# Attention values for four query tiles at once, an 8 KB weight pool, and the query's inverse root multiplied on POOL

## The chip, the cores and the metric

The kernel runs on one core of a Trainium2 chip. The core has five engines with queues of their own: TensorE (PE; its weight loads are shown as PEld), VectorE (DVE), ScalarE (ACT), GpSimd (POOL) and SyncE (SP, which here only issues DMAs). Every engine executes its own instructions in order and waits on semaphores for the others. The metric is the device time of one execution in microseconds.

## What is computed

One encoder layer over 1024 tokens of width 1024, all in float32, in three sub-layers with residuals. The first mixes a bidirectional RG-LRU with a multi-head latent attention of 8 heads (96 columns of query and key, 64 of value); then come a memory cross-attention and a convolutional SwiGLU feed-forward network (FFN). The change is mostly about the latent attention:

```python
q = rms_norm(q, q_norm)
k = rms_norm(k, k_norm)
q = concatenate([q[..., :64], apply_rope(q[..., 64:], cos, sin)])
k = concatenate([k[..., :64], apply_rope(k[..., 64:], cos, sin)])
...
def attend(q_blk):                       # 8 blocks of 128 queries
    s = einsum('bhqd,bhkd->bhqk', q_blk, kh) * 96 ** -0.5
    p = softmax(s, axis=-1)
    return einsum('bhqk,bhkd->bhqd', p, vh)
```

Norm and rotation leave a factor that belongs to the query's row, the inverse root of its mean square. It may be multiplied into the query, or into the row of scores.

## The kernel before

Every float32 operand of a matmul is split into a rounded hi part and the rest, lo, and a product is made of three matmuls (`mm3`: hi·hi, hi·lo, lo·hi). Weights come through the pool `wp`: a `raw` tile (two buffers) is loaded by SP, and `wsplit` (L125) makes hi and lo of it, on POOL (L134 and L135) or on ACT and DVE. Each is a tile of 1024 columns under the tag "w", of which there are twelve. The two gate tiles (`gate_zero`, L181), the transposed memory rows `mT`, the memory's keys and values `kvr`, the transposed probabilities `pT` and the weights of the FFN's last matmul (`dhi`, `dlo`) take slots of the same tag.

The order of the instructions on each engine isn't written by hand. The context is opened with `schedule_with_timeline_sim=True`: a scheduler with a timeline of its own sets it while the program is built. So a change of a pool can move instructions of stages that it doesn't touch. In the first 60 us the kernel normalises and transposes x (hT), loads the pieces of w_in in the order `w_first`, `w_second`, and on, and projects (psin); beside that, POOL works out the decay factors of the RG-LRU (`sp`).

The attention is a loop over 64 turns, 8 heads by 8 query tiles of 128. For a query tile s:

- `scores(s)`: six matmuls into psS (two PSUM buffers of 1024 columns, pool `pb2`). DVE takes the row maximum into `st` (L754) and multiplies it with the query's inverse root `rq` (L756); ACT takes the Exp with that as its bias and `rq` as its scale (L758), and its row sum; DVE takes the reciprocal (L759); POOL scales the probabilities `pr` in place (L760).
- `turn(s)`: PE transposes `pr` in eight blocks into two psT banks (pool `pb1`, four banks in all, which po and the transposes of keys and queries use too); ACT copies the hi part to pT (L776), DVE subtracts for the lo part (L777).
- `values(u, part)`: a unit u is two query tiles. Its 16 matmuls of 256 columns make po, in two parts of eight. ACT copies the hi and lo halves of po to `ot` (L797, L798), and POOL adds them into `mo` (L799).

In the loop, scores run two turns ahead and values two behind. Between the turns, the next head is prepared: `prep_kn` multiplies the key with its inverse root on POOL (L733, L734), `prep_k` and `prep_q` transpose (`tr96`, L712 to L714), and `head_stats` and `head_roots` work out the inverse roots of the next two heads on ACT, DVE (`inv_root`, L545 to L550) and POOL.

Of the kernel before, what the change touches and what calls it, by code (L numbers as in the profile page):

```python
# [21 lines left out]
P = 128  # L22
# [61 lines left out]
def trunk_layer(ctx: ExitStack, tc: tile.TileContext, a: dict, out: bass.AP):  # L84
# [8 lines left out]
    abcd = ExitStack()  # L93
    wp = abcd.enter_context(tc.tile_pool(name="wp", bufs=12, reuse_waits="tile"))
    lrs = ExitStack()
# [29 lines left out]
    def wsplit(raw, n=1024, gains=None, eng="pool"):  # L125
        hi = wp.tile([P, 1024], F32R, tag="w", name="whi")
        lo = wp.tile([P, 1024], F32R, tag="w", name="wlo")
        w = n // len(gains) if gains else n
        for i in range(n // w):
            sl = slice(i * w, (i + 1) * w)  # L130
            if eng == "pool":
                if gains:
                    pool.tensor_scalar(raw[:, sl], raw[:, sl], gains[i], 0.0, ALU.mult, ALU.add)
                pool.tensor_scalar(hi[:, sl], raw[:, sl], 1.0, 0.0, ALU.mult, ALU.add)  # L134
                pool.tensor_sub(lo[:, sl], raw[:, sl], f(hi)[:, sl])  # L135
# [45 lines left out]
    def gate_zero(jj):  # L181

        wg[jj] = wp.tile([P, 1024], F32, tag="w", name="wgate")
        pool.memset(wg[jj], 0.0)
# [408 lines left out]
    def tp_tile(tag, bufs):  # L593
        return lambda shape, name: tp.tile(shape, F32, tag=tag, bufs=bufs, name=name)


    mT = [[wp.tile([P, 4, MEM], F32R, tag="w", name="mT") for _ in range(2)]
          for q in range(2)]

# [59 lines left out]
    def mem_kv_half(n):  # L659
# [12 lines left out]
        for m in range(2):  # L672
            if n == 0:
                kvr.append(wp.tile([P, 1024], F32, tag="w", name="kvr"))
            act.activation(kvr[m][:, n * 512:(n + 1) * 512], pkv[m], AF.Copy)
# [65 lines left out]
    def prep_q(H, n):  # L741
        qTs[H, n] = cp.tile([QKH, 2, 512], F32R, tag="qT", name="qT")
        tr96(hq[H // 2][:, n * 4:n * 4 + 4, H % 2, :], col("q_g")[:QKH], qTs[H, n])

    def scores(s):
# [8 lines left out]
        dve.tensor_reduce(st[:, 0:1], psS, AX.X, ALU.max, negate=True)  # L754
        r = rq[H // 2][:, i, H % 2:H % 2 + 1]
        dve.tensor_scalar(st[:, 1:2], st[:, 0:1], r, None, ALU.mult)  # L756
        pr = cp.tile([P, S], F32, tag="pr", bufs=3, name="pr")
        act.activation(pr, psS, AF.Exp, bias=st[:, 1:2], scale=r, accum_out=st[:, 2:3])  # L758
        dve.reciprocal(st[:, 3:4], st[:, 2:3])  # L759
# [3 lines left out]
    scaled = {}  # L763

    def turn(s):
        qi = s % 2
        if qi == 0:
            pTs[s // 2] = [[wp.tile([P, 4, 2 * P], F32R, tag="w", name="pT") for _ in range(2)] for _ in range(2)]
        pr = prs.pop(s)
        for n in range(2):  # L770
# [3 lines left out]
            pv = ps.rearrange("p (k c) -> p k c", k=4)  # L774
            dh = pTs[s // 2][n][0][:, :, qi * P:(qi + 1) * P]
            act.activation(dh, pv, AF.Copy)  # L776
            dve.tensor_sub(pTs[s // 2][n][1][:, :, qi * P:(qi + 1) * P], pv, f(dh))  # L777

    def values(u, part):

        H, qq = divmod(u, NT // 2)
        p, hh = H // 2, H % 2
        vt = vts[H]
        if part == 0:
            pos_[u] = pb1.tile([P, 512], F32, tag="b1", name="po")
        po = pos_[u][:, :2 * P]
        th, tl = pTs[u][part]
        for k in range(4):
            mm(po, vt[:, part * 4 + k], th[:, k, :], part == 0 and k == 0, False)
            mm(po, vt[:, part * 4 + k], tl[:, k, :], False, part == 1 and k == 3)  # L790
        if part == 0:
            return
        if qq == 0 and hh == 0:
            mla_f[p] = cp.tile([P, S], F32, tag="mo", bufs=2, name="mo")
        mo = mla_f[p]
        ot = cp.tile([P, 2, 2 * P], F32, tag="ot", bufs=1, name="ot")[VD * hh:VD * hh + VD]
        act.activation(ot[:, 0], po[:VD, :], AF.Copy)  # L797
        act.activation(ot[:, 1], po[VD:2 * VD, :], AF.Copy)  # L798
        pool.tensor_add(mo[VD * hh:VD * hh + VD, qq * 2 * P:(qq + 1) * 2 * P], ot[:, 0], ot[:, 1])  # L799
        if qq < NT // 2 - 1 or hh == 0:  # L800
            return
# [19 lines left out]
    for s in range(NQ + 2):  # L821
        H, i = divmod(s, NT)
        if s + 2 < NQ:
            scores(s + 2)
        if s < NQ:
            turn(s)
        if s >= 2:
            values((s - 2) // 2, s % 2)
        with tc.issue_after(scaled[min(s + 1, NQ - 1)].ins):
# [371 lines left out]
    def product(m):  # L1201
# [5 lines left out]
        for i in range(NH):  # L1207
# [66 lines left out]
```

## Time and profile before

| | |
|---|---|
| median of 3 runs | 1427.37 us (1425.83 to 1431.77) |
| profiled execution | 1426.61 us, span 1424.8 us |
| granted PE clock | 0.995 |
| attention | about 262 to 495 us |
| FFN, first and last matmuls | about 754 to 1212 and 1212 to 1425 us |

The times are of whole executions; the profile shows one, with a span that leaves out 1.8 us around it. A page of the profile lists the busy time of each engine, the costliest groups of instructions and the chain of waits that ended last. In a group's row, the name before the arrow is what is written and the names behind it are what is read; behind the bar stand the busy time, the mean of one in ns, and the time that the engine was idle just before these instructions, with the instruction that ended most of it. PE's matmuls overlap, so their mean is longer than the distance from one to the next.

### The profile page before, as it was taken

What the parts mean: (1) busy time and instruction counts of PE and PEld (TensorE: products, weight loads), DVE (VectorE), ACT (ScalarE), POOL (GpSimd) and SP (SyncE); (2) the same over time, 40 slices, a digit from 0 to 9 for tenths busy, and PEclk for the clock granted to TensorE, in tenths of its full rate; (3) what the DMA queues carried; (4) which work ended last, traced back from release to release, by engine and by line L of the source; (5) the groups of instructions that cost most, each with busy time, mean ns of one, the idle gap of its engine ahead of it and who ended that gap; (6) DMA issues with size and microseconds to landing.
All of it is one profiled execution on the core that took longest, in us unless ns stands there. A gap on an engine that the chain in (4) does not pass through costs nothing.

```text
span 1424.8 us, 18309 instructions
## 1 busy us (share of the span) xinstructions
PE 1373.2 (96%) x6832; PEld 1151.6 (81%) x6832; DVE 903.9 (63%) x1242; ACT 601.2 (42%) x954; POOL 562.2 (39%) x591
## 2 busy tenths in 40 slices
PE   6999899998999999999999999999999999999998
PEld 5766698787888888888887888888888888888887
DVE  6678877899998854576645666443443444665553
ACT  5456855687888822454421111111111122433331
POOL 6713474457687610111339998233223300000000
PEclk9999999999999999999999999999999999999999
DMA  6301101100000141101118887321332222666763
GB/s 203 92 24 37 46 31 47 58 1 1 1 1 1 53 169 46 60 1 30 45 62 279 289 300 254 108 96 59 109 98 81 96 77 94 199 224 205 221 192 103
DMA packets 114232, 145.94 MB, mean 102 GB/s; under 512 B 9547, under 2 KB 64096, under 8 KB 114144
## 3 DMA queue, kind: packets, MB, share of 16 engines
q1 hardware_dynamic: 114143, 144.78, 31.4%
q8 instruction: 54, 0.88, 0.3%
q14 instruction: 35, 0.28, 0.1%
HBM read 105.95 MB, written 38.80 MB: 102 GB/s over the span
## 4 chain that ended last, share of the span: by engine, by line
PE 72%; DVE 11%; ACT 7%; POOL 5%; issue 3%; DMA 2%; SPq 1%; POOLq 0%; ACTq 0%; DVEq 0%
PE psup L109 32%; PE psdn L109 8%; PE psdw L109 6%; PE psP L109 6%; PE psq L109 3%; PE psS L109 3%; PE po L109 3%; PE psmo L109 3%; PE psT L773 2%; DVE st L754 2%; DVE pT L777 1%; POOL wlo L135 1%; PE pq L109 1%; ACT pr L758 1%; DMA raw<-in_w_in 1%
## 5 line engine op out<-in xcount | busy, mean ns | idle before, releaser
L109 PE MATMUL psup<-h,whi 128*128 128x512 f32 x1408 | 434.5, 390 | 1.1 <-POOL ws L1188 0.9
L109 PEld LDWEIGHTS psup<-h,whi 128*128 128x128 f32 x1408 | 264.2, 188 | 56.7 <-POOL ws L1188 1.2
L109 PE MATMUL psup<-h,wlo 128*128 128x512 f32 x704 | 274.1, 389 | 0.0
L1162 ACT ACTIVATE gu<-psup,fcw 128x1024 f32<-128x1024 f32 x44 | 53.3, 1212 | 286.2 <-PE psup L109 286.2
L1163 DVE SCALAR_TENSOR_TENSOR gu<-psup,fcw,gu 128x1023 f32<-128x1023 f32 x44 | 56.4, 1281 | 183.7 <-ACT gu L1162 183.7
L1221 DVE TENSOR_TENSOR dlo<-rawd,dhi 128x1024 fp32r<-128x1024 f32 x77 | 93.3, 1223 | 102.2 <-ACT dhi L1220 102.1
L109 PEld LDWEIGHTS psup<-h,wlo 128*128 128x128 f32 x704 | 132.2, 188 | 27.3
L134 POOL TENSOR_SCALAR whi<-raw 128x1024 fp32r<-128x1024 f32 (+2 forms) x58 | 68.2, 1176 | 217.0 <-PE psup L109 178.0
L135 POOL TENSOR_TENSOR wlo<-raw,whi 128x1024 fp32r<-128x1024 f32 (+2 forms) x58 | 142.3, 2454 | 27.8 <-PE psin L109 24.6
L1220 ACT ACTIVATE dhi<-rawd 128x1024 fp32r<-128x1024 f32 x77 | 81.4, 1061 | 158.8 <-PE psdw L109 44.8
L109 PE MATMUL psS<-kT,qT 96*128 96x512 f32 x384 | 103.9, 404 | 3.9 <-ACT pr L758 3.8
L109 PE MATMUL psin<-hT,whi 128*128 128x512 f32 (+1 forms) x288 | 89.0, 393 | 9.5 <-DVE xf L355 8.2
L760 POOL TENSOR_SCALAR pr<-pr,st 128x1024 f32<-128x1024 f32 x64 | 71.8, 1123 | 54.1 <-DVE st L759 32.8
L777 DVE TENSOR_TENSOR pT<-psT,pT 128x512 fp32r<-128x512 f32 x128 | 84.4, 678 | 5.5 <-ACT pT L776 5.4
L758 ACT ACTIVATE pr<-psS,st,rqk 128x1024 f32<-128x1024 f32 x64 | 77.2, 1206 | 18.6 <-DVE st L756 14.2
L754 DVE TENSOR_REDUCE st<-psS 128x1 f32<-128x1024 f32 x64 | 77.6, 1213 | 8.3 <-PE psS L109 6.7
L109 PEld LDWEIGHTS psS<-kT,qT 96*128 96x128 f32 x384 | 67.6, 189 | 17.6 <-ACT pr L758 6.2
L1188 POOL TENSOR_TENSOR ws<-rawd 128x512 f32<-128x512 f32 x55 | 79.4, 1471 | 0.0
L109 PE MATMUL po<-pT,vt 128*128 128x256 f32 x512 | 72.3, 287 | 3.5 <-DVE pT L777 3.3
L776 ACT ACTIVATE pT<-psT 128x512 fp32r<-128x512 f32 x128 | 70.9, 596 | 7.5 <-PE psT L773 6.9
L773 PE MATMUL psT<-ident,pr 128*128 128x128 f32 x512 | 68.3, 273 | 5.7 <-POOL pr L760 3.6
L109 PEld LDWEIGHTS psin<-hT,whi 128*128 128x128 f32 x288 | 54.6, 198 | 23.6 <-issue 6.7
(301 smaller groups left out, 2810.0 us busy)
## 6 DMA issues: line engine op xcount, KB each, us to landing
raw<-in_w_up SPq DMA_DIRECT2D x44, 512.0 KB
rawd<-ad SPq DMA_DIRECT2D x77, 256.0 KB
wd<-ws SPq DMA_DIRECT2D x55, 256.0 KB
ad<-as SPq DMA_DIRECT2D x55, 256.0 KB
rawd<-wd SPq DMA_DIRECT2D x55, 256.0 KB
rawd<-in_w_down SPq DMA_DIRECT2D x22, 512.0 KB
ad<-gu SPq DMA_DIRECT2D x22, 256.0 KB
rawd<-in_w_down SPq DMA_DIRECT2D x22, 256.0 KB
```

The costliest lines, as they stand in the source:

```text
L109: return pe.matmul(ps, lhsT=l, rhs=r, start=start, stop=stop)
L134: pool.tensor_scalar(hi[:, sl], raw[:, sl], 1.0, 0.0, ALU.mult, ALU.add)
L135: pool.tensor_sub(lo[:, sl], raw[:, sl], f(hi)[:, sl])
L754: dve.tensor_reduce(st[:, 0:1], psS, AX.X, ALU.max, negate=True)
L758: act.activation(pr, psS, AF.Exp, bias=st[:, 1:2], scale=r, accum_out=st[:, 2:3])
L760: scaled[s] = pool.tensor_scalar(pr, pr, st[:, 3:4], 0.0, ALU.mult, ALU.add)
L773: pe.transpose(ps[:, i * P:(i + 1) * P], pr[:, (n * 4 + i) * P:(n * 4 + i + 1) * P], ident)
L776: act.activation(dh, pv, AF.Copy)
L777: dve.tensor_sub(pTs[s // 2][n][1][:, :, qi * P:(qi + 1) * P], pv, f(dh))
L1188: pool.tensor_tensor(st, raws[h0][:, c0], raws[h1][:, c1], op)
L1220: act.activation(hi, raw, AF.Copy)
L1221: dve.tensor_sub(lo, raw, f(hi))
```

## The change

There are three edits.

1. The tag "w" of `wp` has six slots of 8 KB a partition in place of twelve of 4 KB. Tiles are allocated in pairs: hi and lo of a weight, both gate tiles, the two tiles of `mT`, of `kvr`, and `dhi` with `dlo`.
2. A unit of the values is four query tiles: 16 matmuls of 512 columns each fourth turn, issued ahead of the transposes of that turn. A pT tile is twice as wide. ACT copies one half of po straight to `mo` and the other to `ot`, and POOL adds `ot` to `mo`.
3. `prep_q` multiplies the query with its inverse root on POOL, in place, ahead of the transposes. The scores then need neither the scale of the Exp nor the multiplied maximum.

```diff
-    wp = abcd.enter_context(tc.tile_pool(name="wp", bufs=12, reuse_waits="tile"))
+    wp = abcd.enter_context(tc.tile_pool(name="wp", bufs=6, reuse_waits="tile"))
...
     def wsplit(raw, n=1024, gains=None, eng="pool"):
-        hi = wp.tile([P, 1024], F32R, tag="w", name="whi")
-        lo = wp.tile([P, 1024], F32R, tag="w", name="wlo")
+        hl = wp.tile([P, 2, 1024], F32R, tag="w", name="whl")
+        hi, lo = hl[:, 0], hl[:, 1]
...
     def gate_zero(jj):
-        wg[jj] = wp.tile([P, 1024], F32, tag="w", name="wgate")
+        if jj == 0:
+            wg["both"] = wp.tile([P, 2, 1024], F32, tag="w", name="wgate")
+        wg[jj] = wg["both"][:, jj]
         pool.memset(wg[jj], 0.0)
...
     def prep_q(H, n):
         qTs[H, n] = cp.tile([QKH, 2, 512], F32R, tag="qT", name="qT")
-        tr96(hq[H // 2][:, n * 4:n * 4 + 4, H % 2, :], col("q_g")[:QKH], qTs[H, n])
+        q = hq[H // 2][:, n * 4:n * 4 + 4, H % 2, :]
+        r = rq[H // 2][:, n * 4:n * 4 + 4, H % 2:H % 2 + 1]
+        pool.tensor_tensor(q, q, r.to_broadcast([P, 4, QKH]), ALU.mult)
+        tr96(q, col("q_g")[:QKH], qTs[H, n])
...
         dve.tensor_reduce(st[:, 0:1], psS, AX.X, ALU.max, negate=True)
-        r = rq[H // 2][:, i, H % 2:H % 2 + 1]
-        dve.tensor_scalar(st[:, 1:2], st[:, 0:1], r, None, ALU.mult)
         pr = cp.tile([P, S], F32, tag="pr", bufs=3, name="pr")
-        act.activation(pr, psS, AF.Exp, bias=st[:, 1:2], scale=r, accum_out=st[:, 2:3])
+        act.activation(pr, psS, AF.Exp, bias=st[:, 0:1], scale=1.0, accum_out=st[:, 2:3])
...
+    NG = 4
+
     def turn(s):
-        qi = s % 2
+        qi = s % NG
         if qi == 0:
-            pTs[s // 2] = [[wp.tile([P, 4, 2 * P], F32R, tag="w", name="pT") for _ in range(2)] for _ in range(2)]
+            pTs[s // NG] = [[wp.tile([P, 4, NG * P], F32R, tag="w", name="pT") for _ in range(2)] for _ in range(2)]
...
-    def values(u, part):
+    def values(u):
...
-        po = pos_[u][:, :2 * P]
-        th, tl = pTs[u][part]
-        for k in range(4):
-            mm(po, vt[:, part * 4 + k], th[:, k, :], part == 0 and k == 0, False)
-            mm(po, vt[:, part * 4 + k], tl[:, k, :], False, part == 1 and k == 3)
-        if part == 0:
-            return
+        po = pb1.tile([P, 512], F32, tag="b1", name="po")
+        for part in range(2):
+            th, tl = pTs[u][part]
+            for k in range(4):
+                mm(po, vt[:, part * 4 + k], th[:, k, :], part == 0 and k == 0, False)
+                mm(po, vt[:, part * 4 + k], tl[:, k, :], False, part == 1 and k == 3)
...
-        ot = cp.tile([P, 2, 2 * P], F32, tag="ot", bufs=1, name="ot")[VD * hh:VD * hh + VD]
-        act.activation(ot[:, 0], po[:VD, :], AF.Copy)
-        act.activation(ot[:, 1], po[VD:2 * VD, :], AF.Copy)
-        pool.tensor_add(mo[VD * hh:VD * hh + VD, qq * 2 * P:(qq + 1) * 2 * P], ot[:, 0], ot[:, 1])
+        hr = slice(VD * hh, VD * hh + VD)
+        mc = mo[hr, qq * NG * P:(qq + 1) * NG * P]
+        ot = cp.tile([P, NG * P], F32, tag="ot", bufs=1, name="ot")[hr]
+        act.activation(mc, po[:VD, :], AF.Copy)
+        act.activation(ot, po[VD:2 * VD, :], AF.Copy)
+        pool.tensor_add(mc, mc, ot)
...
         if s + 2 < NQ:
             scores(s + 2)
+        if s >= NG and s % NG == 0:
+            values(s // NG - 1)
         if s < NQ:
             turn(s)
-        if s >= 2:
-            values((s - 2) // 2, s % 2)
```

The scheduler's order moves with it, at three places that the prediction speaks of. The first is POOL near 28 us, at the second and third piece of w_in (whi and wlo, or whl, are hi and lo; rs is the inverse root of a row of x). Before:

```order
L209 TENSOR_TENSOR xt_113<-xt_113,gba_91 128x1024
L134 TENSOR_SCALAR whi_484<-raw_115 128x1024
L146 TENSOR_TENSOR rs_247<-rs_247,nhalf_80 128x1
L146 TENSOR_TENSOR rs_268<-rs_268,nhalf_80 128x1
L135 TENSOR_TENSOR wlo_485<-raw_115,whi_484 128x1024
L134 TENSOR_SCALAR whi_549<-raw_547 128x1024
L135 TENSOR_TENSOR wlo_550<-raw_547,whi_549 128x1024
```

The same place on POOL with the change:

```order
L211 TENSOR_TENSOR xt_112<-xt_112,gba_91 128x1024
L134 TENSOR_SCALAR whl_483<-raw_114 128x1024
L146 TENSOR_TENSOR rs_246<-rs_246,nhalf_80 128x1
L146 TENSOR_TENSOR rs_267<-rs_267,nhalf_80 128x1
L134 TENSOR_SCALAR whl_547<-raw_545 128x1024
L135 TENSOR_TENSOR whl_483<-raw_114,whl_483 128x1024
L135 TENSOR_TENSOR whl_547<-raw_545,whl_547 128x1024
```

The hi of the third piece now stands ahead of the lo of the second. The memset of the second gate tile, which stood between the fifth and the sixth piece, has moved to the start of POOL's queue, and the gate's eight DMAs on SP ahead of the load of the fourth piece.

The second place is DVE in the first head of the attention. Before:

```order
L754 TENSOR_REDUCE st<-psS 128x1
L549 SCALAR_TENSOR_TENSOR t_2276<-t_2276 128x16
L759 RECIPROCAL st<-st 128x1
L777 TENSOR_TENSOR pT<-psT,pT 128x4x128
L756 TENSOR_SCALAR st<-st,rqk 128x1
L550 SCALAR_TENSOR_TENSOR rqk<-t_2276 128x2x8
L777 TENSOR_TENSOR pT<-psT,pT 128x4x128 x2
```

DVE there with the change (L760 is the maximum, L763 the reciprocal, L783 the subtraction for pT):

```order
L760 TENSOR_REDUCE st<-psS 128x1
L783 TENSOR_TENSOR pT<-psT,pT 128x4x128
L763 RECIPROCAL st<-st 128x1
L551 SCALAR_TENSOR_TENSOR t_2859<-t_2859 128x16
L717 SCALAR_TENSOR_TENSOR qT<-ps_2442,pcols,qT 96x512
L783 TENSOR_TENSOR pT<-psT,pT 128x4x128 x2
```

The multiply of the maximum, which stood three instructions behind it, is gone; what follows the maximum no longer stands ahead of the Exp.

The third is PE in the middle of the attention, for one unit of values. Before:

```order
L109 MATMUL po<-pT,vt 128x256 x9
L109 MATMUL psS<-kT,qT 128x512 x6
L109 MATMUL po<-pT,vt 128x256 x7
L773 MATMUL psT<-ident,pr 128x128 x8
L712 MATMUL ps_3841<-ident,kn 96x128 x4
L109 MATMUL psS<-kT,qT 128x512 x6
```

PE with the change:

```order
L109 MATMUL po<-pT,vt 128x512
L109 MATMUL psS<-kT,qT 128x512 x6
L779 MATMUL psT<-ident,pr 128x128 x4
L109 MATMUL po<-pT,vt 128x512 x8
L779 MATMUL psT<-ident,pr 128x128 x4
L109 MATMUL po<-pT,vt 128x512 x7
L109 MATMUL psS<-kT,qT 128x512 x6
L779 MATMUL psT<-ident,pr 128x128 x8
```

A unit's values are still 16 matmuls, of twice the columns and half as often; scores and transposes of a turn stand between their pieces. On POOL, the 16 new multiplies (L748) stand in pairs: six ahead of the first scaled probabilities, then two each behind the 4th, 11th and 15th and four behind the 43rd and 46th together.

More of the change, by code (lines that the diff above doesn't have):

```diff
@@ L594, in tp_tile @@
         return lambda shape, name: tp.tile(shape, F32, tag=tag, bufs=bufs, name=name)
-    mT = [[wp.tile([P, 4, MEM], F32R, tag="w", name="mT") for _ in range(2)]
-          for q in range(2)]
+    mT = [wp.tile([P, 2, 4, MEM], F32R, tag="w", name="mT") for q in range(2)]
+    mT = [(t[:, 0], t[:, 1]) for t in mT]
     def mem_rows(m):
@@ L672, in mem_kv_half @@
         for m in range(2):
-            if n == 0:
-                kvr.append(wp.tile([P, 1024], F32, tag="w", name="kvr"))
+            if n == 0 and m == 0:
+                kvt = wp.tile([P, 2, 1024], F32, tag="w", name="kvr")
+                kvr.extend((kvt[:, 0], kvt[:, 1]))
             act.activation(kvr[m][:, n * 512:(n + 1) * 512], pkv[m], AF.Copy)
@@ L774, in turn @@
             pv = ps.rearrange("p (k c) -> p k c", k=4)
-            dh = pTs[s // 2][n][0][:, :, qi * P:(qi + 1) * P]
+            dh = pTs[s // NG][n][0][:, :, qi * P:(qi + 1) * P]
             act.activation(dh, pv, AF.Copy)
-            dve.tensor_sub(pTs[s // 2][n][1][:, :, qi * P:(qi + 1) * P], pv, f(dh))
-    def values(u, part):
-        H, qq = divmod(u, NT // 2)
+            dve.tensor_sub(pTs[s // NG][n][1][:, :, qi * P:(qi + 1) * P], pv, f(dh))
+    def values(u):
+        H, qq = divmod(u, NT // NG)
         p, hh = H // 2, H % 2
         vt = vts[H]
-        if part == 0:
-            pos_[u] = pb1.tile([P, 512], F32, tag="b1", name="po")
-        po = pos_[u][:, :2 * P]
-        th, tl = pTs[u][part]
-        for k in range(4):
-            mm(po, vt[:, part * 4 + k], th[:, k, :], part == 0 and k == 0, False)
-            mm(po, vt[:, part * 4 + k], tl[:, k, :], False, part == 1 and k == 3)
-        if part == 0:
-            return
+        po = pb1.tile([P, 512], F32, tag="b1", name="po")
[4 more added lines that the diff above has]
+                mm(po, vt[:, part * 4 + k], tl[:, k, :], False, part == 1 and k == 3)
         if qq == 0 and hh == 0:
@@ L795, in values @@
         mo = mla_f[p]
-        ot = cp.tile([P, 2, 2 * P], F32, tag="ot", bufs=1, name="ot")[VD * hh:VD * hh + VD]
-        act.activation(ot[:, 0], po[:VD, :], AF.Copy)
-        act.activation(ot[:, 1], po[VD:2 * VD, :], AF.Copy)
-        pool.tensor_add(mo[VD * hh:VD * hh + VD, qq * 2 * P:(qq + 1) * 2 * P], ot[:, 0], ot[:, 1])
-        if qq < NT // 2 - 1 or hh == 0:
+        hr = slice(VD * hh, VD * hh + VD)
[4 more added lines that the diff above has]
+        pool.tensor_add(mc, mc, ot)
+        if qq < NT // NG - 1 or hh == 0:
             return
@@ L1217, in product @@
             nc.sync.dma_start(raw[:, 0], ad[m, i])
-            hi = wp.tile([P, 2, 512], F32R, tag="w", name="dhi")
-            lo = wp.tile([P, 2, 512], F32R, tag="w", name="dlo")
+            hl = wp.tile([P, 2, 2, 512], F32R, tag="w", name="dhl")
+            hi, lo = hl[:, 0], hl[:, 1]
             act.activation(hi, raw, AF.Copy)
```

## The prediction

> **What bounds the kernel now.** The page's first part gives busy shares over the whole span:
>
> ```profile
> PE 1373.2 (96%) x6832; PEld 1151.6 (81%) x6832; DVE 903.9 (63%) x1242; ACT 601.2 (42%) x954; POOL 562.2 (39%) x591
> ```
>
> TensorE (PE) is busy for 96% of the span, so a change pays only if it shortens PE's own work or the few microseconds in which PE waits. Edits 2 and 3 work in the attention, which the trace has from about 262 to 495 us. There the windows view (core 0: stretch and its length, then busy time and count of PE, PEld, DVE, ACT and POOL, PE clock, DMA share, GB/s) says how close the other engines are:
>
> ```profile
> core 0: us, PE busy (x) PEld busy (x) DVE busy (x) ACT busy (x) POOL busy (x), PEclk, DMA share, GB/s
> ...
> 300.00:340.00 40.00, 35.86 (x246) 31.57 (x244) 38.10 (x75) 32.45 (x61) 24.88 (x35) 1.00 0.00 1
> 340.00:380.00 40.00, 38.85 (x265) 34.60 (x266) 37.05 (x75) 33.65 (x62) 28.88 (x40) 1.00 0.01 1
> 380.00:420.00 40.00, 36.97 (x249) 32.57 (x248) 38.42 (x80) 32.30 (x61) 34.47 (x49) 1.00 0.00 1
> ```
>
> VectorE (DVE) is busy 37 to 38 of 40 us, and where it reaches 38, PE falls to 36 or 37: PE and DVE share the bound. The groups of that stretch (262 to 495 us; after the bar: busy us, mean ns of one, idle us of the engine just before them and its releasers; a few records are missing, the code has 384, 512, 512 and 64) show what the waits are:
>
> ```profile
> L109 PE MATMUL psS<-kT,qT 96*128 96x512 f32 x372 | 100.8, 405 | 3.9 <-ACT pr L758 3.8
> L777 DVE TENSOR_TENSOR pT<-psT,pT 128x512 fp32r<-128x512 f32 x126 | 83.0, 678 | 5.4 <-ACT pT L776 5.2
> L758 ACT ACTIVATE pr<-psS,st,rqk 128x1024 f32<-128x1024 f32 x64 | 77.2, 1206 | 18.6 <-DVE st L756 14.2 <-DVE t L548 1.9 <-DVE t L546 1.2
> ...
> L109 PE MATMUL po<-pT,vt 128*128 128x256 f32 x495 | 69.6, 288 | 3.5 <-DVE pT L777 3.3
> L773 PE MATMUL psT<-ident,pr 128*128 128x128 f32 x508 | 67.7, 273 | 5.7 <-POOL pr L760 3.6 <-DVE pT L777 1.4 <-ACT ot L798 0.7
> ...
> L799 POOL TENSOR_TENSOR mo<-ot 64x256 f32<-64x256 f32 x30 | 22.5, 750 | 8.8 <-ACT ot L798 4.8 <-PE psT L773 3.1
> ...
> L756 DVE TENSOR_SCALAR st<-st,rqk 128x1 f32<-128x1 f32 x62 | 12.4, 200 | 0.1
> ...
> L733 POOL TENSOR_TENSOR kn<-hp,rqk 128x256 f32<-128x256 f32 x12 | 7.5, 621 | 5.5 <-PE ps L712 5.2
> ...
> L734 POOL TENSOR_TENSOR kn<-krs,rqk 128x128 f32<-128x128 f32 x12 | 4.8, 404 | 0.0
> ```
>
> PE's idle time in the attention is 3.9 + 5.7 + 3.5 = 13.1 us; most of it waits for the Exp (L758) or the scaled probabilities that follow it (L760). The Exp itself idles 18.6 us, and 14.2 of that ends with L756, the small multiply that edit 3 removes. This is the wait that matters.
>
> **Edit 2, the value matmuls.** 512 matmuls of 256 columns become 256 of 512. The chain of waits has undisturbed rows of either width (start, duration, count), and of scores and transposes, needed later:
>
> ```profile
> 284.62 1.39 PE psS L109 x6
> 286.01 1.31 PE psT L773 x12
> ...
> 402.39 1.89 PE po L109 x16
> ...
> 754.49 457.21 PE psup L109 x2016
> ```
>
> A 256-column matmul takes 1.89 / 16 = 118 ns, a 512-column one 457.21 / 2016 = 227 ns (scores: 1.39 / 6 = 232). So 512 x 118 = 60.5 us become 256 x 227 = 58.1: **-2.4 us** of PE work. [...] ACT's and POOL's evictions of the values become half as many at twice the width. The 16 POOL adds of 512 columns take at most twice the 0.75 us of L799, 24 us as now; ACT saves fixed costs, and is not the bound.
>
> **Edit 3, the removed multiply and the new one.** L756 takes 0.2 us, 64 times, 12.8 us of DVE at most. Worse is where it stands. DVE and ACT around 281 us (start, duration):
>
> ```profile
> 280.02 1.21 DVE L754 TENSOR_REDUCE st<-psS 128x1 f32<-128x1024 f32 x1
> ...
> 281.15 0.16 DVE L550 SCALAR_TENSOR_TENSOR t<-t 128x16 f32<-128x16 f32 x1
> 281.24 0.15 DVE L759 RECIPROCAL st<-st 128x1 f32<-128x1 f32 x1
> 281.31 0.66 DVE L777 TENSOR_TENSOR pT<-psT,pT 128x512 fp32r<-128x512 f32 x1
> ...
> 281.90 0.20 DVE L756 TENSOR_SCALAR st<-st,rqk 128x1 f32<-128x1 f32 x1
> ...
> 282.19 1.20 ACT L758 ACTIVATE pr<-psS,st,rqk 128x1024 f32<-128x1024 f32 x1 [2.53 <-DVE st L756]
> ```
>
> The maximum is there at 281.23, but three other DVE instructions are queued between it and L756, and the Exp starts at 282.19. It could have started some 0.1 us behind the maximum (L756 starts at 281.90, lasts 0.20, and the Exp follows 0.09 later): 0.87 us earlier. The order of the instructions has one to three such instructions between nearly every maximum and its L756, often the reciprocal, which itself waits for the Exp before. After the change the Exp waits for the maximum alone. Bounds: nothing, if PE then waits for something else, and all 13.1 us. Of these, 3.9 + 5.7 hang on the Exp and what follows it, and 3.5 on L777, which loses only the 0.2 us ahead of it. I take about nine tenths of the first 9.6: **-8.5 us**. What is late next is DVE itself: 38 of 40 us less 11 turns x 0.2 us (a turn is 233 / 64 = 3.6 us) leaves 36, just under PE's share.
>
> The new POOL multiply has 128x384 elements, 16 times. Rows L734 and L733 give 0.404 us for 128 columns and 0.621 for 256; another 128 by the same step make 0.84 us, 13.4 us in all. POOL has room for it in the first two windows. But four of the 16 stand together behind the 43rd and 46th scaled tile, in the stretch around 380 to 420 us, where POOL is busy 34.47 of 40 us: 34.5 + 4 x 0.84 = 37.8. The scaling of the next tile is queued behind them, and PE's transposes wait for that; the transposes of the query wait for the multiply itself, a new wait. Between 0 (POOL idles enough) and 3.4 us (all four show) I take **+1.0 us**.
>
> One row speaks against more POOL work:
>
> ```profile
> 282.68 0.15 DVE L548 TENSOR_TENSOR t<-rqk,t 128x16 f32<-128x16 f32 x1
> ...
> 323.62 1.13 POOL L760 TENSOR_SCALAR pr<-pr,st 128x1024 f32<-128x1024 f32 x1 [0.53 <-DVE t L545]
> 323.76 1.00 DVE L548 TENSOR_TENSOR t<-rqk,t 128x16 f32<-128x16 f32 x1
> ```
>
> The same small DVE instruction took 0.15 us once and 1.00 us while POOL ran L760, and both ended together. [...]
>
> **Edit 1, the weight pool.** Twelve pieces of 4 KB become six of 8 KB, so a weight's hi and lo share a slot, and so do both gate tiles. The order after shows what that moves, in the first 62 us. POOL now writes the hi of the third weight ahead of the lo of the second. The trace of before at that place (POOL, one DMA of the chain of waits, and ACT at the end):
>
> ```profile
> 27.74 1.05 POOL L134 TENSOR_SCALAR whi<-raw 128x1024 fp32r<-128x1024 f32 x1
> ...
> 29.17 3.98 DMA raw<-in_w_in
> ...
> 29.79 2.54 POOL L135 TENSOR_TENSOR wlo<-raw,whi 128x1024 fp32r<-128x1024 f32 x1
> ...
> 33.23 1.04 POOL L134 TENSOR_SCALAR whi<-raw 128x1024 fp32r<-128x1024 f32 x1 [0.90 <-DMA raw<-in_w_in]
> ...
> 34.36 2.40 POOL L135 TENSOR_TENSOR wlo<-raw,whi 128x1024 fp32r<-128x1024 f32 x1
> ...
> 40.74 1.05 POOL L134 TENSOR_SCALAR whi<-raw 128x1024 fp32r<-128x1024 f32 x1 [0.51 <-DMA raw<-in_w_in]
> ...
> 45.30 0.96 POOL L184 MEMSET wgate<- 128x1024 f32 x1
> ...
> 61.82 0.20 POOL L311 TENSOR_SCALAR sp<-sp 128x8 f32<-128x8 f32 x1
> 62.05 1.24 ACT L388 ACTIVATE av<-thr,sp 128x1024 f32<-128x1024 f32 x1 [8.85 <-POOL sp L311]
> ```
>
> The third weight's DMA lands only at 33.15, so its hi cannot start before 33.23. The lo that ran at 29.79 in POOL's idle time now runs at 34.4 to 36.8, and the third lo to 39.2. Only the end of the second's lo frees its raw buffer: the load issued then (before: 32.3; after: 36.8) lands 4.0 us later, at 40.8. Then hi (1.05) and lo (2.4) of the fourth end at 44.3, where the next hi starts, not at 40.74: 3.6 us late. The second gate memset (0.96) has moved ahead to where POOL idled, so 2.6 remain on POOL's queue until sp, for which ACT waits 8.85 us at 62. The eight gate DMAs that moved ahead of the fourth weight's load on SP's queue take 0.63 us each and are through before its buffer is free. From 62 us on, nothing is fixed in time that could take the shift back: **+2.6 us**, between 0 (other slack) and 4.
>
> **Sum**, against the profiled execution's 1426.6 us (span 1424.8 and 1.8 around it; 0.8 below the median 1427.4): 1426.6 + 2.6 - 2.4 - 8.5 + 1.0 = **1419.3 us**. The out projection, memory attention and FFN, with PE busy throughout, stay as they are.
>
> **Rivals.**
> - All 13.1 us of PE's waits go and POOL costs nothing: 1426.6 + 2.6 - 2.4 - 13.1 = 1413.7. For it: 14.2 us of waits at L756 vanish at their source. Against it: DVE stays nearly as busy as PE.
> - It doesn't do what it says: the Exp starts earlier, but DVE is as busy with the rest and PE's waits move elsewhere. 1426.6 + 2.6 - 2.4 = 1426.8.
> - The slower side: the lump. Values come as 16 matmuls of 3.6 us every fourth turn. In the three turns between, PE has 1.39 + 8 x 0.109 = 2.26 us of work and DVE 1.21 + 2 x 0.68 + 0.15 = 2.72: PE idles 0.46 x 3 = 1.4 us, unless DVE has worked ahead during the lump, which two score buffers allow only in part. It cancels the gain from 0.46 us a unit (7.3 / 16), and at half of 1.4, 11 us over 16 units, with no gain at the Exp, gives 1426.6 + 2.6 - 2.4 + 11 = 1437.8. For it: before, half as large a lump came twice as often. Against it: the order splits it in 9 + 7 or 8 + 7 with transposes or scores between.
>
> **How the numbers follow.** Forecast 0.50, full recovery 0.18, no recovery 0.17, the lump 0.15. About 0.5%, 7.1 us, is what a measurement of this kernel tells from no change: faster means below 1420.2, slower above 1434.5. The forecast's own spread (8.5 by 4 us either way, the early shift by 1.5) puts 0.3 of its 0.5 below 1420.2. Faster: 0.3 + 0.17 = 0.47; same: 0.2 + 0.01 + 0.17 = 0.38; slower 0.15. The range 1409 to 1437 leaves out the ends of the full recovery and of the lump.
>
> **What would show it.** The profile after should have no DVE instruction between maximum and Exp, under 5 us of ACT idle before the Exp, PE idle in the attention near 5 us, value rows near 227 ns apart, and sp about 2.6 us later. Wrong it would be if DVE's busy share stays at 38 of 40 us, if PE idles before psT for POOL, or if PE's idle time sits in the turns without values.

## The result, and the profile after

The changed kernel takes **1450.5 us** (median; 1447.8 to 1451.0) where the kernel before takes 1426.7. The ratio is 1.015, with an interval of 1.012 to 1.017: slower by 24 us, where 7 us faster was forecast, and outside the range of 1409 to 1437. Single slow executions, of 1544 to 3546 us, are left out of all medians below.

The first part of the page (busy us, share of the span, instructions), after:

```profile
PE 1386.3 (96%) x6576; PEld 1142.9 (79%) x6576; DVE 893.7 (62%) x1178; ACT 590.0 (41%) x922; POOL 570.7 (39%) x591
```

It reads almost like the one of before. Places show more than shares. From the timelines and the chains of waits, start of the same instruction in the two traces:

| | before, us | after, us | later by |
|---|---|---|---|
| a row of the up projection (pk, six matmuls) | 204.69 | 210.21 | 5.5 |
| first Exp of the attention | 261.23 | 267.78 | 6.6 |
| 45th Exp | 423.50 | 430.25 | 6.8 |
| 49th Exp | 438.71 | 455.46 | 16.8 |
| 64th (last) Exp | 489.69 | 510.85 | 21.2 |
| out projection, a row of 156 matmuls | 513.14 | 537.34 | 24.2 |
| FFN, the row of 2016 matmuls | 754.49 | 778.58 | 24.1 |

Everything is lost by the start of the out projection, and most of it at three places: 5.5 us ahead of the up projection, 10.0 in the four turns between the 45th and 49th Exp, and 7.4 from there to the out projection. From the first to the 45th Exp both kernels take the same time (162.3 us before, 162.5 after), so the three edits together gained nothing there either.

The groups after, 268 to 515 us, columns as before:

```profile
L783 DVE TENSOR_TENSOR pT<-psT,pT 128x512 fp32r<-128x512 f32 x122 | 80.2, 682 | 30.2 <-ACT pT L782 20.7 <-PE po L109 9.4
L762 ACT ACTIVATE pr<-psS,st 128x1024 f32<-128x1024 f32 x64 | 71.9, 1123 | 14.5 <-DVE st L763 8.4 <-DVE st L760 6.0
L782 ACT ACTIVATE pT<-psT 128x512 fp32r<-128x512 f32 x123 | 68.1, 604 | 30.5 <-PE psT L779 30.1
L109 PE MATMUL psS<-kT,qT 96*128 96x512 f32 x372 | 103.6, 410 | 5.2 <-ACT pr L762 4.8
L779 PE MATMUL psT<-ident,pr 128*128 128x128 f32 x504 | 70.0, 277 | 5.5 <-POOL pr L764 2.6 <-DVE pT L783 1.3 <-ACT ot L803 1.0
L109 PE MATMUL po<-pT,vt 128*128 128x512 f32 x240 | 67.1, 415 | 0.9 <-DVE kT L717 0.5 <-DVE qT L717 0.3
L715 PE MATMUL ps<-ident,kn 128*96 128x128 f32 x56 | 8.9, 283 | 6.8 <-POOL kn L737 6.0 <-DVE t L550 0.8
```

ACT idles 14.5 us ahead of the Exp, not under 5. Its copies of the transposed probabilities now idle 30.5 us, 30.1 of them for PE. On the page of before it was 7.5:

```profile
L776 ACT ACTIVATE pT<-psT 128x512 fp32r<-128x512 f32 x128 | 70.9, 596 | 7.5 <-PE psT L773 6.9
```

DVE's share did fall as forecast, to 33 to 36 of 40 us in the windows from 300 to 420 us. PE's idle time in these rows is 5.2 + 5.5 + 0.9 + 6.8 = 18.4 us, against 13.1 before, and the last row is new: transposes of a key that wait for its scaling on POOL. The windows view (columns as before) and the timeline (start, duration, the wait in brackets) of that place:

```profile
430.00:440.00 10.00, 4.78 (x25) 3.32 (x23) 9.79 (x19) 4.20 (x8) 8.09 (x10) 0.86 0.00 0
440.00:450.00 10.00, 7.95 (x34) 7.05 (x35) 4.33 (x11) 4.14 (x7) 5.54 (x9) 0.63 0.01 2
```

```profile
401.52 1.05 ACT L588 ACTIVATE acct<-mo 128x1024 f32<-128x1024 f32 x1
404.15 2.82 POOL L593 TENSOR_TENSOR acc<-acc,acct 128x256 f32<-128x256 f32 x4
407.69 0.66 ACT L562 ACTIVATE sqk<-hp 128x512 f32<-128x512 f32 x1
...
427.26 0.63 ACT L562 ACTIVATE sqk<-hp 128x512 f32<-128x512 f32 x1
...
429.99 0.60 PE L715 MATMUL ps<-ident,kn 128*96 128x128 f32 x4
...
440.76 0.17 DVE L552 SCALAR_TENSOR_TENSOR rqk<-t 128x16 f32<-128x16 f32 x1
441.02 0.62 POOL L736 TENSOR_TENSOR kn<-hp,rqk 128x256 f32<-128x256 f32 x1 [2.21 <-DVE rqk L552]
441.59 0.40 POOL L737 TENSOR_TENSOR kn<-krs,rqk 128x128 f32<-128x128 f32 x1
442.05 1.09 PE L715 MATMUL ps<-ident,kn 128*96 128x128 f32 x4 [5.97 <-POOL kn L737]
```

PE waits 5.97 us for a key of the last pair of heads, whose inverse roots are ready only at 440.9. The same places in the trace of before:

```profile
393.83 0.16 DVE L550 SCALAR_TENSOR_TENSOR rqk<-t 128x16 f32<-128x16 f32 x1
394.08 1.06 ACT L586 ACTIVATE acct<-mo 128x1024 f32<-128x1024 f32 x1 [0.38 <-DVE st L759]
...
400.16 0.63 ACT L560 ACTIVATE sqk<-hp 128x512 f32<-128x512 f32 x1
...
424.67 0.16 DVE L550 SCALAR_TENSOR_TENSOR rqk<-t 128x16 f32<-128x16 f32 x1
```

The squares of the finished second pair (L586, L588), the statistics (sqk) and the temporaries of the inverse roots (t) share one buffer, the tile acct. Before, the first half of the last pair's statistics and roots was through it at 394.0, then came the squares. With the change, the values are written ahead of the turn, so the squares claim the buffer first, and both halves follow: the second ends at 440.9, not 424.8, where the Exps up to there are only 6.8 us late.

### The profile page after: what moved, and what is told of

Same layout as the page of the kernel before. It is cut to its first block, busy times and chain, and to the rows that moved or that the text cites. A ratio compares the mean times of both kernels' runs of the same rounds, so it can differ in the third digit from the quotient of the medians.

```text
span 1448.9 us, 17645 instructions
## 1 busy us (share of the span) xinstructions
PE 1386.3 (96%) x6576; PEld 1142.9 (79%) x6576; DVE 893.7 (62%) x1178; ACT 590.0 (41%) x922; POOL 570.7 (39%) x591
## 4 chain that ended last, share of the span: by engine, by line
PE 72%; DVE 12%; ACT 9%; POOL 3%; issue 3%; DMA 1%; SPq 1%; ACTq 0%; POOLq 0%; DVEq 0%
PE psup L109 33%; PE psdn L109 8%; PE psdw L109 6%; PE psP L109 6%; PE po L109 4%; PE psq L109 3%; PE psmo L109 3%; PE psS L109 2%; DVE st L760 2%; DVE pT L783 2%; PE psT L779 1%; ACT pT L782 1%; ACT pr L762 1%; PE pq L109 1%; DMA raw<-in_w_in 1%
## 5 line engine op out<-in xcount | busy, mean ns | idle before, releaser
L109 PE MATMUL psup<-h,whl 128*128 128x512 f32 x2112 | 480.7, 389 | 1.1 <-DVE gu L1169 0.9
L109 PEld LDWEIGHTS psup<-h,whl 128*128 128x128 f32 x2112 | 396.2, 188 | 84.0 <-POOL ws L1193 1.2
L135 POOL TENSOR_TENSOR whl<-raw,whl 128x1024 fp32r<-128x1024 f32 (+2 forms) x58 | 144.8, 2498 | 3.3
L1226 DVE TENSOR_TENSOR dhl<-rawd,dhl 128x1024 fp32r<-128x1024 f32 x77 | 93.3, 1223 | 73.0 <-ACT dhl L1225 73.0
L1225 ACT ACTIVATE dhl<-rawd 128x1024 fp32r<-128x1024 f32 x77 | 81.3, 1060 | 117.0 <-PE psdw L109 46.4
L109 PE MATMUL psdn<-dhl 128*128 128x512 f32 x528 | 120.3, 389 | 0.0
L109 PEld LDWEIGHTS psdn<-dhl 128*128 128x128 f32 x528 | 99.1, 188 | 20.5
L109 PE MATMUL psin<-hT,whl 128*128 128x512 f32 (+1 forms) x432 | 101.4, 393 | 13.8 <-DVE xf L357 8.6
L109 PEld LDWEIGHTS psin<-hT,whl 128*128 128x128 f32 x432 | 79.4, 200 | 33.8 <-issue 11.8
L783 DVE TENSOR_TENSOR pT<-psT,pT 128x512 fp32r<-128x512 f32 x128 | 84.0, 682 | 32.4 <-ACT pT L782 23.0
L109 PE MATMUL psdw<-dhl 128*128 128x512 f32 x396 | 90.2, 389 | 0.0
L109 PEld LDWEIGHTS psdw<-dhl 128*128 128x128 f32 x396 | 74.3, 188 | 15.4
L760 DVE TENSOR_REDUCE st<-psS 128x1 f32<-128x1024 f32 x64 | 77.8, 1216 | 7.5 <-PE psS L109 7.3
L762 ACT ACTIVATE pr<-psS,st 128x1024 f32<-128x1024 f32 x64 | 71.9, 1123 | 14.5 <-DVE st L763 8.4
```

The source lines that it names most:

```text
L109: return pe.matmul(ps, lhsT=l, rhs=r, start=start, stop=stop)
L762: act.activation(pr, psS, AF.Exp, bias=st[:, 0:1], scale=1.0, accum_out=st[:, 2:3])
L783: dve.tensor_sub(pTs[s // NG][n][1][:, :, qi * P:(qi + 1) * P], pv, f(dh))
L1226: dve.tensor_sub(lo, raw, f(hi))
```

## The experiments

The theories. Time is lost at places of their own: at the buffer acct and in the early part that edit 1 reorders (letter A in the expectations, where one is named). Rivals: the new multiplies fill POOL and hold up the scaled tiles (D); edit 2 itself costs, by its block of 16 wide value matmuls and the order of the queues that comes with it (C); the probabilities lack a slot (H). Where an expectation gives a letter another meaning, it says so. Each ratio compares a kernel with runs of before that were made beside it. Their medians were 1426.9 to 1427.4, and they spread from 1425 to 1437, so a ratio can differ by 0.1 or 0.2% from that of two medians.

**1. Squares of a finished pair one turn later** (behind the first half of the statistics, as before):

```diff
+        if p < 3:
+            held.append((p, mo))
+        else:
+            pair_done(p, mo)
...
+        if held and s % NG == 1:
+            pair_done(*held.pop())
```

> The changed kernel, with the squares of a finished pair of heads (and what hangs on them) issued one turn later, so that the first half of the statistics of the next pair is again ahead of them in the queue for the single acct tile. Theory A (the acct tile: since values come a turn earlier, the square of the second pair takes the tile before the statistics of the fourth pair, which then start some 10 turns late, and the keys of head 6 are late): the 10 us lost between the 44th and 48th Exp go, PE's 6.0 us wait for kn goes, total about 1440. Rival B (the lump of 16 value matmuls or the fuller POOL starves the others there): no change, about 1450, and the wait stays.

Measured 1440.2 us (ratio 1.008, 1.006 to 1.010): 10.4 less. The key's row in the groups:

```profile
L715 PE MATMUL ps<-ident,kn 128*96 128x128 f32 x56 | 8.5, 273 | 0.8 <-DVE t L550 0.8
```

Its idle time fell from 6.8 to 0.8 us with all multiplies still on POOL, and from the 45th to the 49th Exp it takes 15.0 us (15.2 before, 25.2 in the changed kernel). The order at acct was the cause of these 10 us.

**2 to 4. One edit alone, or one left out.** Edit 1 alone; edit 3 alone; edits 1 and 2 without 3. None needs a line that the diff doesn't have.

> The kernel before with edit 1 alone (six slots of 8 KB, hi and lo in one, pT's hi and lo in one). Theory A (edit 1 costs only in the first 62 us, by POOL's order there, and the shift grows by a collision of POOL and DVE at about 72 us): +5 us at the queries' up projection, about 1432 in all, attention as before. Rival C (the early shift is hidden or comes from the other edits): 1427.

> The kernel before with edit 3 alone (the query multiplied on POOL, no multiply of the maximum). Theory A (the Exp waits for the maximum alone, 13 us of PE's waits are there to be had): 1418 to 1423, PE idle in the attention under 9 us, sp at 62 us as before. Rival D (POOL's 13.4 us of multiplies and its collisions with DVE eat it): 1427 or more.

> The changed kernel without edit 3 (the maximum is multiplied on DVE again, no multiply of the query on POOL): edits 1 and 2 alone. Theory A (the stall near the 44th turn is the acct tile's, and has nothing to do with the multiplies): it stays, some 1450 to 1455. Rival D (the multiplies that stand behind the 43rd scaled tile on POOL make it): the stall goes, 1435 to 1440.

Edit 1 alone: 1437.2 us (1.005, 1.003 to 1.007), twice the loss expected; its up projection is 6.4 us late, the rest is lost in the attention. Edits 1 and 2: 1456.6 us (1.019, 1.016 to 1.023); the squares go first without the multiplies too, and the four turns from the 45th to the 49th Exp take 20.9 us, so POOL's extra work isn't the cause of the stall. Edit 3 as a whole saves 6.1 us beside them (1456.6 - 1450.5). Edit 3 alone: 1432.0 us (1.0029, 1.0013 to 1.0046), not faster but slower. Its groups, 262 to 515 us:

```profile
L774 PE MATMUL psT<-ident,pr 128*128 128x128 f32 x512 | 71.9, 276 | 8.0 <-DVE pT L778 5.9 <-DVE kT L714 2.1
L777 ACT ACTIVATE pT<-psT 128x512 fp32r<-128x512 f32 x128 | 74.8, 598 | 22.7 <-PE psT L774 22.0
L759 ACT ACTIVATE pr<-psS,st 128x1024 f32<-128x1024 f32 x62 | 69.3, 1118 | 15.4 <-DVE st L757 9.1 <-DVE st L760 3.3 <-DVE t L546 1.5
```

The multiply and its wait are gone (14.2 us before), but ACT still idles 15.4 ahead of the Exp, now mostly for the maximum itself (L757), and 22.7 ahead of the copies, where it was 7.5. The timeline shows how, at one place:

```profile
369.58 1.22 DVE L757 TENSOR_REDUCE st<-psS 128x1 f32<-128x1024 f32 x1 [0.46 <-PE psS L109]
...
371.13 1.04 PE L774 MATMUL psT<-ident,pr 128*128 128x128 f32 x8
...
371.77 1.08 ACT L777 ACTIVATE pT<-psT 128x512 fp32r<-128x512 f32 x2 [1.13 <-PE psT L774]
...
372.74 1.12 ACT L759 ACTIVATE pr<-psS,st 128x1024 f32<-128x1024 f32 x1
```

The maximum is done at 370.80. The Exp stands on ACT behind two copies that wait for PE, and starts 1.94 us later. At this place the head of ACT's queue waits for something else now. It is one place, and most of the loss lies elsewhere: from the 36th to the 48th Exp this kernel takes 50.6 us and the one before 42.4, and the inverse roots of the last pair's second half are ready at 433.5 in place of 424.8.

**5. Values in two pieces.** Experiment 1, with the second half of a unit's values held behind the next turn's transposes:

```diff
         if s >= NG and s % NG == 0:
-            values(s // NG - 1)
+            values(s // NG - 1, 0)
         if s < NQ:
             turn(s)
+        if s > NG and s % NG == 1 or s == NQ + 1:
+            with tc.issue_after(last_tr[min(s, NQ - 1)].ins):
+                values(s // NG - 1, 1)
```

> As the first experiment (all three edits, squares one turn later), with a unit's 16 value matmuls in two parts: eight in the turn in which they came, and eight held on PE behind the transposes of the next turn. Theory C (the lump: with 16 value matmuls of 512 columns in one turn PE has too little work in the other three, which costs about 1 us a unit where PE sets the pace): the heads without statistics fall from 29 to 30 us to 28 to 28.5, total 1428 to 1433 (from 1440). Rival F (it isn't the lump but POOL's multiplies and the order on ACT, where copies for pT now stand ahead of a ready Exp): 1438 to 1442.

Measured 1449.1 us (1.014, 1.011 to 1.017): 9 worse than in one piece. The four tiles' probabilities stay in use a turn longer that way, so this neither supports nor rules out the block as a cause.

**6. The early order of before.** Experiment 1, with the two gate tiles apart and the hi of w_in's third piece kept behind the lo of the second:

```diff
+                if len(los) == 1:
+                    with tc.issue_after(los[0].ins):
+                        pool.tensor_scalar(hi[:, sl], raw[:, sl], 1.0, 0.0, ALU.mult, ALU.add)
...
-        if jj == 0:
-            wg["both"] = wp.tile([P, 2, 1024], F32, tag="w", name="wgate")
-        wg[jj] = wg["both"][:, jj]
+        wg[jj] = wp.tile([P, 2, 1024], F32, tag="w", name="wgate")[:, 0]
```

> As the first experiment, with the order of the first 62 us as before: the gate tiles apart (each half an 8 KB slot), and POOL's hi of the third piece of w_in held behind the lo of the second. Theory A (the shift of 5.4 us at the queries' up projection comes from that order alone; POOL's late piece then also stretches DVE's multiply at 72 us): ACT starts av at 62.0 again, the up projection at 204.7, total about 1435. Rival G (pairs of hi and lo cost something wherever they are, or the pool of six starves a load): shift of over 3 us stays, 1438 or more.

Measured 1435.0 us (1.004, 1.003 to 1.006): 5.2 less, and the row of the up projection stands at 204.77, as before. That the early order cost these 5 us is shown. It isn't quite the order of before, though: the factor av, which waits for sp, starts at 58.93 here and not at 62.05, and yet the up projection comes no earlier. So the start of av alone doesn't set it.

**7 to 10. Edits 1 and 3, bare and mended; edit 3 mended; hi first.** "Mended" is with the order of experiment 6 where edit 1 is there, and with the squares two turns later, behind both halves of the statistics. Hi first is experiment 1 with each part's four hi matmuls ahead of its four lo ones. The two changes:

```diff
+        if held and s % 4 == 2:
+            pair_done(*held.pop())
```

```diff
             for k in range(4):
                 mm(po, vt[:, part * 4 + k], th[:, k, :], part == 0 and k == 0, False)
+            for k in range(4):
                 mm(po, vt[:, part * 4 + k], tl[:, k, :], False, part == 1 and k == 3)
```

> The kernel before with edits 1 and 3, values still by two tiles. If the costs of edit 1 (9.8 us) and of edit 3 (4.6 us) add up: 1442, and the wider values, with squares one turn later, are then worth 2 us (1440 in the first experiment). Theory C (the lump costs over 5 us more than the wider matmuls save): 1435 or less.

> As the first experiment, with the eight matmuls of each part of a unit's values in another order: the four of hi, then the four of lo (before: alternating), so that the hi tile of a part is free four matmuls, 0.9 us, earlier. Theory H (five of the six slots are pT's, one is kvr's; a unit needs four, so its last tile takes the hi slot of the other unit's second part, and DVE and ACT wait there for value matmuls): DVE's waits for po fall from 3.9 us to under 1, total 1436 to 1438. Rival C (the lump itself holds the transposes back, slots or not): 1440, or slower.

> Edits 1 and 3 with values by two tiles, the order of the first 62 us as before (as in the sixth experiment), and the squares of a finished pair two turns later, so that both halves of the statistics are ahead of them. Theory A: 5.3 us from the first 62 us and 3 to 4 us from head 5 (33.0 us, whose second half of statistics waits for acct) off 1433.5: 1423 to 1426, faster than before by 1 to 4 us. Rival G (the costs only move on): 1428 to 1434.

> Edit 3 alone on the kernel before, with the squares two turns later as in the run ahead of this. Edit 3 alone lost 8.4 us between the 36th and the 48th Exp, where the second half of the fourth pair's statistics waits for acct. Theory A (that wait is the loss): 1423 to 1426. Rival D (it is POOL's multiplies and the order on ACT): 1430 to 1433 as in the third experiment.

| | us | ratio |
|---|---|---|
| edits 1 and 3 | 1433.5 | 1.0041 (1.0028 to 1.0055) |
| experiment 1, hi first | 1436.8 | 1.0055 (1.0035 to 1.0074) |
| edits 1 and 3, mended | 1426.2 | 0.9988 (0.9972 to 1.0005) |
| edit 3, mended | 1424.3 | 0.9963 (0.9943 to 0.9982) |

The losses of the edits don't add: 9.8 for edit 1 alone and 4.6 for edit 3 alone (against 1427.4), but 6.5 for both (against 1427.0); and edit 2, with the squares moved, costs 6.7 beside them (1440.2 - 1433.5). Hi first gains 3.4 us beside experiment 1. DVE's wait for value matmuls ahead of its subtraction, 3.9 us there, is gone; but the order moved elsewhere too, so the gain can't be laid to one wait. Mended, both edits are even with the kernel before, and edit 3 alone is the one version that measured faster than it, by 0.4%, inside the 0.5% that counted as no change. Moving the squares took the stall away: from the 36th to the 48th Exp it takes 42.7 us. Its profiled execution, the longest of its twelve, is no shorter than that of before (span 1425.2 us, before 1424.8), so the trace doesn't show where the gain lies.

**11. A sixth slot for the probabilities.** One of the six 8 KB slots holds the memory's projected keys and values (kvr) during the attention. Here kvr is filled with ones after the attention, so the memory's own keys and values are left out, and the slot is free. Beside experiment 1:

```diff
+        kvs = wp.tile([P, 1024], F32, tag="raw", bufs=2, name="kvs")
         for m in range(2):
-            act.activation(kvr[m][:, n * 512:(n + 1) * 512], pkv[m], AF.Copy)
+            act.activation(kvs[:, m * 512:(m + 1) * 512], pkv[m], AF.Copy)
...
+    kvt = wp.tile([P, 2, 1024], F32, tag="w", name="kvr")
+    kvr.extend((kvt[:, 0], kvt[:, 1]))
+    for m in range(2):
+        pool.memset(kvr[m], 1.0)
```

> As the first experiment, with the slot of kvr free during the attention: the memory's projected keys and values go to a raw tile and are dropped, and kvr is filled with ones behind the attention (this leaves out the memory's own keys and values). pT then has six slots. Theory H (slots): heads without statistics fall below 28.5 us, DVE's waits for po go, total 1432 to 1435 (1440 in the first experiment). Rival C (the lump): 1438 to 1441, heads at 29 to 30 us as there.

Measured 1440.5 us (1.008, 1.005 to 1.010), as experiment 1. DVE's wait for value matmuls is gone here too, without a gain. The order moved with it (the first Exp comes at 257.2 and not at 267.4, the last at 502.2 and 501.4), so this speaks against the slots and doesn't rule them out.

**12. All three edits, mended, hi first.**

> All three edits, with everything that helped: early order as in the sixth experiment (-5.2), hi matmuls first as in the eighth (-3.4), squares two turns later. If these add: 1440.2 - 5.2 - 3.4 = 1431.6, less up to 2 for the second half of the statistics: 1429 to 1432, so edit 2 still costs 3 to 6 us beside the ninth run (1426.2). Rival: 1426 or less, the wider values cost nothing once slots and order are right.

Measured 1432.1 us (1.0019, 1.0004 to 1.0034), as expected: 6.0 above the mended kernel without edit 2 (1426.2), which hasn't hi first. The windows view from the first Exp to the out projection's row of 156 matmuls, without edit 2:

```profile
261.72:511.13 249.41, 239.44 (x1604) 212.07 (x1603) 210.50 (x366) 195.44 (x370) 172.13 (x228) 1.00 0.07 24
```

and with it:

```profile
262.37:519.14 256.77, 244.87 (x1348) 198.12 (x1347) 207.14 (x366) 188.53 (x338) 171.75 (x212) 0.99 0.07 23
```

The stretch is 7.4 us longer, with 256 matmuls fewer. PE's open idle time grew by 1.9 us (9.97 to 11.90) and its "busy" time by 5.4 (239.44 to 244.87). The profile models the ends of matmuls; whether short waits for an operand are counted in that, it doesn't show.

**13 and 14. Width or block.** First, two tiles' 16 narrow matmuls (256 columns) in one block every second turn, without edit 2; then the kernel of experiment 12 with a unit's values as two halves of 256 columns, 32 narrow matmuls in one block:

```diff
-        if s >= 2:
-            values((s - 2) // 2, s % 2)
+        if s >= 2 and s % 2 == 0:
+            values((s - 2) // 2, 0)
+            values((s - 2) // 2, 1)
```

```diff
-        for part in range(2):
...
+        for c in (slice(0, 2 * P), slice(2 * P, 4 * P)):
+            for part in range(2):
...
+                    mm(po[:, c], vt[:, part * 4 + k], th[:, k, c], part == 0 and k == 0, False)
```

> Edits 1 and 3 with both mends (1426.17 us), with the 16 value matmuls of two tiles issued together in every second turn in place of 8 in each. The size of the block is the cost: some of edit 2's 6 us show here, 1428 to 1432. Only a block of four tiles, or wide matmuls, cost: 1425 to 1427.5, as without this edit.

> All three edits with both mends and hi first (1432.14 us), with a unit's values as two halves of 256 columns, one after the other: 32 matmuls of half the width in one block. Wide matmuls are the cost: the time falls to that of the kernels without edit 2, 1425 to 1429. The block of four tiles is the cost: 2.4 us of matmul work come back and nothing else changes, 1432 to 1437.

Measured 1428.6 us (0.9998, 0.9985 to 1.0012) and 1436.6 us (1.0053, 1.0034 to 1.0072). Another form, with each wide matmul as two narrow ones side by side, gave no time. Two tiles in one block cost 2.4 us beside 1426.2; by the ratios it is 1.4, with intervals that overlap, so this difference isn't clear. Four tiles with narrow matmuls cost 4.4 us more than with wide ones, and not less. So the width is not the cost of edit 2. How much it saves isn't shown, since the form with two halves also keeps the probabilities of a unit in use until the second half. Four tiles at once, narrow, stand 10.4 us above two by two (1436.6 - 1426.2; 9.3 by the ratios).

Is it the length of the block on PE? The traces speak against it, because the scheduler's order isn't that of the code. PE without edit 2 (edits 1 and 3, mended), and with it (experiment 12):

```profile
337.93 2.14 PE L109 MATMUL po<-pT,vt 128*128 128x256 f32 x16
...
347.57 2.16 PE L109 MATMUL po<-pT,vt 128*128 128x256 f32 x16
```

```profile
360.10 1.11 PE L109 MATMUL po<-pT,vt 128*128 128x512 f32 x4
361.13 1.66 PE L109 MATMUL psS<-kT,qT 96*128 96x512 f32 x6
...
362.99 2.11 PE L109 MATMUL po<-pT,vt 128*128 128x512 f32 x8
364.94 0.60 PE L783 MATMUL psT<-ident,pr 128*128 128x128 f32 x4
365.29 1.18 PE L109 MATMUL po<-pT,vt 128*128 128x512 f32 x4
```

Without edit 2, where the code has blocks of 8, 17 of the 32 units run as one row of 16 all the same (27 in experiment 13). With it, a unit's 16 run in one row only once; most rows have 4 or 8, and 8 wide ones take about as long as 16 narrow ones (2.11 and 2.14 us above). So what costs when the values of four tiles come at once is not shown: it may be the other work that is gathered with them, the order, or how long the probabilities are kept.

## Why the prediction was wrong, point by point

- **Edit 3, "-8.5 us", "after the change the Exp waits for the maximum alone": this step failed.** It does so in its operands, but not in its queue. Alone, edit 3 cost 4.6 us in place of gaining 7.5 (8.5 less 1.0 for POOL). Most of that difference is acct again: the new order delayed statistics there, and mended it measures 1424.3 in place of 1432.0. What is left of the 8.5 is some 3 us (1427.0 - 1424.3; 5 by the ratio), and no trace lays it to the removed wait. In the mended trace PE's open idle time in the attention did fall, to 8.1 us (0.9 + 5.4 + 1.8) from 13.1, but from the first to the last Exp it takes 230.0 us, and the kernel before 228.5. ACT's idle time moved from the Exp (18.6 us before, 13.6 mended) to the copies that wait for PE (7.5 before, 21.1 mended). The bound "nothing, if PE then waits for something else" was in the text; nine tenths was not worked out from a row.
- **The largest part is a term that the prediction put at nothing: acct.** It followed the values on PE, ACT and POOL, but not what is issued behind them in the code. Writing the values ahead of the turn moved the squares of the second pair, which end `values`, ahead of the first half of the last pair's statistics, and the second half came 16 us later (424.8 to 440.9): 10.4 us, the largest single part (experiment 1). A moved step moves every instruction that it issues, and the prediction counted them only as far as the evictions.
- **Edit 1, "+2.6 us": right at sp, too small a size behind it.** The factor av starts at 64.59 and not at 62.05, 2.54 us later. But "nothing is fixed in time" was taken to mean that the shift stays as it is. It grew to 5.5 at the up projection. The first part of that is POOL's lo subtraction, which now meets DVE. After:

```profile
70.70 3.21 POOL L135 TENSOR_TENSOR whl<-raw,whl 128x1024 fp32r<-128x1024 f32 x1
71.72 3.28 DVE L396 TENSOR_TENSOR thi<-thi,thr 128x1024 f32<-128x1024 f32 x1
```

  Before, the two lay apart:

```profile
65.90 2.35 POOL L135 TENSOR_TENSOR wlo<-raw,whi 128x1024 fp32r<-128x1024 f32 x1
69.36 1.22 DVE L394 TENSOR_TENSOR thi<-thi,thr 128x1024 f32<-128x1024 f32 x1
```

  The same DVE instruction took 1.22 us apart from POOL and 3.28 beside it, and by its end the shift is 4.42 us (75.00 and 70.58); where the rest of the 5.5 comes from is not shown. The prediction has a like pair of rows in the attention (L548, 0.15 us and 1.00 beside POOL's L760), but held it against the new multiplies alone; it mattered here. With the early order undone, 5.2 us came back (experiment 6). Edit 1 alone costs 9.8 us; what it costs behind the up projection, no run takes apart.
- **Edit 2, "-2.4 us" of PE work.** On the chain of waits after, most rows of 7 to 9 wide matmuls have 0.23 to 0.27 us each, near the 0.227 taken, and the kernel with narrow ones in their place took 4.4 us more (experiment 14). The evictions came out as said: an ACT copy of 512 columns took 0.59 us, one of 256 columns 0.38, and POOL's adds 1.28 and 0.75. The term stands as work, but not as time: what comes with four tiles at once outweighs it, and edit 2 costs 6.0 us net with hi first (experiment 12), and 8.8 in the order of the code (1435.0 - 1426.2, with the squares one turn later and not two).
- **The lump, the rival with 0.15,** was right that edit 2 costs more than it saves. Its price of 11 us lies near the 10.4 of four tiles at once with narrow matmuls, but its mechanism, 16 matmuls in one row on PE, is not shown: its own reason against, that "the order splits it in 9 + 7 or 8 + 7", holds in the trace. That the two figures meet may be luck, and even this rival stood 13 us below the result. Why edit 2 costs (the transposes on PE, or copies and subtractions that then come in bunches) stays open; cutting the values late (experiment 5) did not help.
- **POOL, "+1.0 us"**, and that four multiplies crowd the next tile: no run takes the multiplies out by themselves. Leaving out edit 3 as a whole made the kernel slower by 6, and PE's wait for the scaled tiles is 2.6 us in the rows after and 3.6 before, so these rows don't point at POOL.
- **"The out projection stays as it is"** is right for its matmuls, whose row of 156 takes 35.49 us in both traces. But between the last Exp and that row lie 26.49 us after and 23.45 before. It isn't edit 2 by itself: in the mended kernels the stretch is 23.81 us with it and 23.91 without. What the 3 us are is not shown. FFN adds nothing.

The parts as the runs give them, one step behind the other: 10.4 (acct) + 5.2 (early order) + 2.8 (hi first and the squares a turn later still, experiment 6 to 12) + 6.0 (edit 2 beside the other edits, mended) = 24.4 us, from 1450.5 to 1426.2, where the kernel before has 1426.7. By the ratios the four are 9.6, 5.7, 3.1 and 4.4. The first two are shown with their place in the trace. Of the last two the runs show the size and not the cause.

## What to carry to other kernels

Where a step is written earlier, follow everything that it issues down to the buffers it claims: at acct, a pool with one buffer, the users came in the order of the code in the traces of before and after, and the squares, moved ahead, held up the statistics that they passed, far from the step itself (roots at 440.9 and not 424.8, with the Exps 6.8 us late). A wait taken from one instruction of a queue may be worth less than it looks (in experiment 3 the Exp stood behind two copies until 1.94 us after its maximum): look at what stands ahead of it and when that is ready. Fewer and wider matmuls are less work in the rows (0.227 us for 512 columns, 0.118 for 256), but gathering more tiles for them moves all that hangs on them, and here all of edit 2 cost 6.0 us net (experiment 12); measure the gathering apart from the width, and read from the trace what the scheduler made of the block.

## What the runs showed of the hardware

- TensorE's granted clock was 0.86 and then 0.63 in the two windows of 10 us around the idle 5.97 us (shown above), where it is 1.00 in the windows of 40 us from 300 to 420. In windows of 1 us it was 1.00 from 430 to 437, 0.59 in the next, 0.50 in each from 438 to 447, then 0.79, and 1.00 from 448 to 456: it fell less than 2 us into the idle stretch, which began at 436.08, and rose more than 5 us behind its end at 442.05. The four transposes behind the wait took 1.09 us, and four like them 0.60 at 429.99. So this place cost more than the idle stretch itself; that the idleness lowered the clock is not shown by one place.
- The DVE instruction `thi<-thi,thr`, which took 1.22 us apart from POOL, took 3.28 us beside POOL's subtraction. It ended at 75.00, 1.09 us behind POOL (70.70 + 3.21 = 73.91).
